# The first feed-forward product of layer 2 in seven block products instead of eight

## The chip, the cores and the metric

The kernel runs on one core of a Trainium2 chip. A core has a matrix engine (TensorE, PE in the profile), a vector engine (VectorE, DVE), a scalar engine (ScalarE, ACT), a general engine (GpSimd, POOL) and a queue that issues transfers (SyncE, SP). The metric is the device time of one execution in microseconds (us), lower is better. Each time is a median over several executions.

## The reference

One inference step of a trunk with two layers, over 512 sample tokens and 128 prompt tokens of width 1024. Each layer has a mixer (layer 1: gated DeltaNet and Hyena, layer 2: two kinds of attention) and then a gated feed-forward part, which is what the change touches in layer 2:

```python
D_MODEL, D_FF = 1024, 2816

def conv_ffn(h, w_up, conv_w, conv_b, w_down):
    a, b = jnp.split(h @ w_up, 2, axis=-1)
    a = dwconv(a, conv_w, conv_b)            # three taps along the tokens
    return (jax.nn.silu(a) * b) @ w_down

        h = rmsnorm(x, p['norm_ffn'][i]) * (1.0 + sc2) + sh2
        x = x + g2 * conv_ffn(h, p['ffn_w_up'][i], ...)
    y = rmsnorm(x, p['final_norm'])
```

"The first feed-forward product" is `h @ w_up`: 640 tokens by 1024 features, times 1024 by 5632 weights. All inputs are float32.

## The kernel before

Everything is feature-major: features on the 128 partitions, tokens along the free axis, in 642 columns (512 sample tokens, two zero columns, 128 prompt tokens). The tokens are worked in two halves, of 384 and 258 columns (`HALVES`; `CHALVES` has 384 and 260, with the neighbours that a three-tap convolution needs). 1024 features are eight tiles of 128, called d or k.

Float32 products are made of three float32r products: an operand is split into a high part (ScalarE casts it, L295) and a low part (VectorE subtracts, L296), and `mm3` (L301 to L303) adds high x high, high x low and low x high. So a weight block of 1024 x 128 (a "w", 512 KB, loaded by SP into one of three buffers named `wr`) costs one cast and one subtraction, and its product with a half of the tokens costs 8 x 3 = 24 matmuls. There is room for four split weights, two pools of two.

`ffn` (L469 to L505) goes over 22 tiles of 128 columns of D_FF, in three groups of 8, 7 and 7 (`FGROUPS`). In each tile (I call it a unit) it makes the a part and the b part of `h @ w_up` (96 matmuls: for a and for b, for either half, 24), convolves a on ScalarE (L512) and VectorE (L518), applies SiLU on ScalarE (L490), multiplies by b on VectorE (L492), and splits the result into `g` (cast on ScalarE L494, subtraction on GpSimd L495). After a group, `project_out` (L434 to L464) adds the group's part of the second product to the residual stream x.

The input of `ffn` comes from the `project_out` before it, that of the mixer. Its last four feature tiles are done for the first half of the tokens and then for the second. While the second is being multiplied, the first half's norm is computed (`norm_stats` L363, `norm_mod` L390 to L403: L394 normalises on VectorE, L400 scales on ScalarE, L402 and L403 split into `h3h` and `h3l`, the low parts on VectorE and GpSimd by turns). The second half's norm follows. `ffn` covers it: it begins with the first half's products of two units (`firsts`, L476), 96 matmuls of 384 columns, and only then needs the second half.

The code is recorded by a framework that assigns each tile its buffer, orders the instructions of each engine once, when the program is built, and adds the semaphores. On the chip ScalarE, VectorE and GpSimd each work through a fixed list in order, and so do TensorE's products. A product group accumulates in one of the eight banks of PSUM (three named "mm", one "s", four "d").

## Time and profile before

| | |
|---|---|
| median of 3 runs | 1935.4 us (1934.53 to 1935.5) |
| the profiled execution, span | 1938.0 us |
| of it: TensorE busy | 1856.1 us |
| VectorE busy | 1168.4 us |
| ScalarE busy | 705.3 us |
| GpSimd busy | 390.2 us |
| first matmul of layer 2's `ffn` | at 1449.54 us |

The profile is of one execution. Its span is 2.6 us above the median of the three timed runs. No time outside the span is listed. A row of a timeline has the start, the duration, the engine, the source line, and what it writes and reads; x2 means that two instructions stand in one row. A row of the groups by line ends with the busy time, the mean duration of one in ns, and the idle time of the engine before them with what ended it. Matmuls overlap in the pipeline, so the step from one to the next is read from their starts, not from their durations.

### The profile page before, as it was taken

How to read it: one execution, taken by the hardware profiler on the slowest of the kernel's cores; microseconds unless marked ns; L12 is line 12 of the kernel's file. 1: busy time of each engine (PE TensorE's matmuls, PEld its weight loads, DVE VectorE, ACT ScalarE, POOL GpSimd, SP SyncE). 2: the span in 40 equal slices, each digit the busy share in tenths (PEclk: the TensorE clock that was granted, in tenths of full speed). 3: DMA queues.
4: the chain of work that ended last, by engine and by line, in shares of the span. 5: the costliest groups of instructions: out<-in, count | busy, mean ns of one | idle time of the engine just before them, and what ended most of it. 6: DMA issues, size and time to landing. Idle time of an engine off the chain costs nothing. (4 is left out here: it accounts for less than half of the span.)

```text
span 1938.0 us, 31344 instructions
## 1 busy us (share of the span) xinstructions
PE 1856.1 (96%) x12512; PEld 1735.8 (90%) x12512; DVE 1168.4 (60%) x2416; ACT 705.3 (36%) x1304; POOL 390.2 (20%) x403
## 2 busy tenths in 40 slices
PE   5899999999888999999999999999999999999998
PEld 1578999998667999999999998978799999999997
DVE  5755666667887669757677648655655433333334
ACT  3555443343222263312312224544435322322332
POOL 2323332324554011101100104310002100110111
PEclk9899999999989999999999999999999999999999
DMA  8321112116552435434344223201212222222221
GB/s 288 126 101 66 44 57 78 56 63 209 167 165 91 142 134 192 135 128 142 119 153 131 70 89 108 82 25 47 88 55 87 68 75 77 74 69 77 74 67 55
DMA packets 66188, 197.48 MB, mean 102 GB/s; under 512 B 6872, under 2 KB 18520, under 8 KB 65914
## 3 DMA queue, kind: packets, MB, share of 16 engines
q1 hardware_dynamic: 52000, 176.71, 28.0%
q10 hardware_dynamic: 14042, 18.76, 2.8%
q8 instruction: 99, 1.62, 0.3%
q14 instruction: 47, 0.39, 0.1%
HBM read 178.91 MB, written 16.54 MB: 101 GB/s over the span
## 5 line engine op out<-in xcount | busy, mean ns | idle before, releaser
L295 ACT CAST wwh<-wr 128x1024 fp32r<-128x1024 f32 (+1 forms) x180 | 185.3, 1029 | 455.2 <-PE mm L302 444.5
L296 DVE TENSOR_TENSOR wwl<-wr,wwh 128x1024 fp32r<-128x1024 f32 (+1 forms) x180 | 221.8, 1232 | 106.8 <-ACT wwh L295 106.7
L302 PE MATMUL mm<-h1l,wwh 128*128 128x384 f32 (+2 forms) x704 | 219.7, 312 | 0.9 <-DVE h1l L403 0.9
L302 PE MATMUL mm<-h3l,wwh 128*128 128x384 f32 (+2 forms) x704 | 219.1, 311 | 0.9 <-DVE h3l L403 0.9
L303 PE MATMUL mm<-h1h,wwl 128*128 128x384 f32 (+2 forms) x704 | 219.5, 312 | 0.0
L301 PE MATMUL mm<-h1h,wwh 128*128 128x384 f32 (+2 forms) x704 | 219.0, 312 | 0.0
L303 PE MATMUL mm<-h3h,wwl 128*128 128x384 f32 (+2 forms) x704 | 218.9, 311 | 0.0
L301 PE MATMUL mm<-h3h,wwh 128*128 128x384 f32 (+2 forms) x704 | 218.3, 311 | 0.0
L518 DVE SCALAR_TENSOR_TENSOR cv<-mm,par,cv 128x259 f32<-128x259 f32 (+3 forms) x272 | 148.6, 548 | 112.9 <-ACT cv L512 110.2
L419 DVE SCALAR_TENSOR_TENSOR x<-mm,mod,x 128x128 f32<-128x128 f32 (+1 forms) x192 | 78.5, 436 | 180.8 <-PE mm L303 180.7
L247 DVE SCALAR_TENSOR_TENSOR mjunk<-mraw,crow 128x512 f32<-128x512 f32 x192 | 150.0, 793 | 2.7 <-ACT crow L235 1.5
L301 PE MATMUL mm<-h0h,wwh 128*128 128x384 f32 (+2 forms) x448 | 148.8, 332 | 0.5 <-DVE d L642 0.2
L302 PE MATMUL mm<-h0l,wwh 128*128 128x384 f32 (+2 forms) x448 | 140.8, 314 | 0.0
L303 PE MATMUL mm<-h0h,wwl 128*128 128x384 f32 (+2 forms) x448 | 139.7, 312 | 0.0
L302 PEld LDWEIGHTS mm<-h1l,wwh 128*128 128x128 f32 x704 | 133.6, 190 | 1.8 <-DVE h1l L403 1.6
L302 PEld LDWEIGHTS mm<-h3l,wwh 128*128 128x128 f32 x704 | 133.1, 189 | 1.8 <-DVE h3l L403 1.6
L303 PEld LDWEIGHTS mm<-h1h,wwl 128*128 128x128 f32 x704 | 133.4, 189 | 0.0
L301 PEld LDWEIGHTS mm<-h1h,wwh 128*128 128x128 f32 x704 | 133.0, 189 | 0.2 <-ACT h1h L402 0.2
L301 PEld LDWEIGHTS mm<-h3h,wwh 128*128 128x128 f32 x704 | 132.8, 189 | 0.2 <-ACT h3h L402 0.2
L303 PEld LDWEIGHTS mm<-h3h,wwl 128*128 128x128 f32 x704 | 132.8, 189 | 0.0
L512 ACT ACTIVATE cv<-mm,par 128x383 f32<-128x383 f32 (+1 forms) x136 | 73.8, 542 | 149.5 <-PE mm L303 144.0
L492 DVE TENSOR_TENSOR fs<-mm,fs 128x384 f32<-128x384 f32 x88 | 42.8, 490 | 98.6 <-PE mm L303 97.6
(462 smaller groups left out, 4657.9 us busy)
## 6 DMA issues: line engine op xcount, KB each, us to landing
wr<-in_w_up SPq DMA_DIRECT2D x88, 512.0 KB, 3.3
wr<-in_w_mod SPq DMA_DIRECT2D x48, 512.0 KB, 4.8
mraw<-in_w_modT SPq DMA_DIRECT2D x48, 512.0 KB, 3.8
wr<-in_w_in SPq DMA_DIRECT2D x28, 512.0 KB, 3.3
wr<-in_w_dn SPq DMA_DIRECT2D x32, 448.0 KB, 3.3
wr<-in_w_out SPq DMA_DIRECT2D x16, 512.0 KB, 3.3
wr<-in_w_dn SPq DMA_DIRECT2D x16, 512.0 KB, 3.6
wr<-in_od_w_in SPq DMA_DIRECT2D x16, 512.0 KB, 3.9
```

What stands on the lines that cost most here:

```text
L247: nc.vector.scalar_tensor_tensor(out=junk, in0=raw[:, c], scalar=1.0, in1=rows[m][:, c], op0=ALU.mult, op1=ALU.mult, accum_out=part[:, d, ...
L295: nc.scalar.copy(hi[:, :K], src)
L296: nc.vector.tensor_tensor(out=lo[:, :K], in0=src, in1=hi[:, :K].bitcast(F32), op=ALU.subtract)
L301: nc.tensor.matmul(ps, l[0](k), r[0](k), start=start, stop=False)
L302: nc.tensor.matmul(ps, l[0](k), r[1](k), start=False, stop=False)
L303: nc.tensor.matmul(ps, l[1](k), r[0](k), start=False, stop=stop)
L419: nc.vector.scalar_tensor_tensor(out=xt[:, a:b], in0=ps[:, a - c0 : b - c0], scalar=mcol(layer, ch, d, m), in1=xt[:, a:b], op0=ALU.mult, o ...
L492: nc.vector.tensor_tensor(out=s[:, a:b], in0=ps[:, : b - a], in1=s[:, a:b], op=ALU.mult)
L512: nc.scalar.activation(t[:, o0:o1], p[:, o0 - a : o1 - a], AF.Identity, scale=w[1], bias=0.0 if bias is None else bias)
L518: nc.vector.scalar_tensor_tensor(out=t[:, c0:c1], in0=p[:, c0 + s_ - a : c1 + s_ - a], scalar=w[i], in1=t[:, c0:c1], op0=ALU.mult, op1=ALU ...
```

## The change

In layer 2 alone, `h` (tokens by features) is taken as 2 x 2 blocks: 320 columns of tokens (0 to 319, or 320 to 511 and the prompt) by four feature tiles. The weights of a unit are 2 x 2 blocks as well: the upper and lower 512 rows of the a part (w11, w21) and of the b part (w12, w22). In place of the eight block products, seven are made, of sums and differences of blocks on either side. Each block product is 4 x 3 = 12 matmuls of 320 columns, so a unit has 84 matmuls.

- `norm_blocks` replaces `norm_mod` here: it normalises as before, scales into four raw blocks (a11, a12, a21, a22), splits a11 and a12 with the first half, and with the second half forms s1 to s4 in four VectorE operations for each k, and splits s1 to s4 and a22. A product of a11 or a12 needs the first half alone. All others need the second.
- `block_weights` splits seven 512 x 128 operands of a unit, and makes four sums of weight blocks on VectorE. Two operands share the room of one split weight, so eight fit.
- `up_unit` makes the seven products in the order a11, a12, s2, s1, s3, s4, a22, in three banks: X takes a11, s2, s3 and a22, one added to the other; V takes s1 and s4; Y takes a12. Between two products into one bank ScalarE copies the running sum out (`keep`: q1, u2, q5, u3). VectorE (two) and GpSimd (two) add the copies up into `ar` and `br`.
- `give` does what followed in `ffn`: the convolution now reads `ar` from SBUF and is three instructions of 641 or 642 columns, in place of six on the halves.
- `ffn_blocks` loops over the units; it begins with a11 and a12 of the first two units.
- `ys` (the output's tiles) are allocated later, tile by tile. `mm3` has a flag that changes no instruction. A scratch size of the build is set to 1024. Comments are dropped, which moves lines: `mm3` is L304 to L306 after the change.

```diff
+SPARTS = (((0, 320, 0),), ((320, 512, 0), (PO, NT, 192)))
+ST = 320
...
+        def split(self, n, k, src, eng=None):
+            if n not in self.hi:
+                self.hi[n], self.lo[n] = (slot(n + t_, (P, 4, ST), F32R) for t_ in "hl")
+            h_ = self.hi[n][:, k, :]
+            nc.scalar.copy(h_, src)
+            (eng or nc.vector).tensor_tensor(out=self.lo[n][:, k, :], in0=src, in1=h_.bitcast(F32), op=ALU.subtract)
...
+    def norm_blocks(x, rb, layer, w, B, hf):
...
+            nc.vector.tensor_tensor(out=t[:, c0:c1], in0=x[d // 2][:, d % 2, c0:c1], in1=rb[:, c0:c1], op=ALU.mult)
...
+                        nc.scalar.activation(
+                            to[:, o + a_ - a : o + b_ - a], t[:, a_:b_], AF.Identity,
+                            scale=scl[:, layer, w, d, m : m + 1], bias=mcol(layer, 0 if w == 0 else 3, d, m),
+                        )
+        if hf == 0:
+            for d in range(KD):
+                norm(d)
+                n = ("a11", "a12")[d // 4]
+                B.split(n, d % 4, B.raw(n, d % 4), nc.vector if d % 2 == 0 else nc.gpsimd)
+            return
+        for k in range(4):
+            norm(k)
+            norm(k + 4)
+            a11, a12, a21, a22 = (B.raw(n, k) for n in ("a11", "a12", "a21", "a22"))
+            s1 = tmp.tile([P, NT], F32, tag="fs", name=nm("s1"))[:, :ST]
+            nc.vector.tensor_tensor(out=s1, in0=a22, in1=a21, op=ALU.subtract)
+            nc.vector.tensor_tensor(out=a11, in0=a11, in1=a21, op=ALU.subtract)
+            nc.vector.scalar_tensor_tensor(out=a21, in0=a11, scalar=-1.0, in1=a22, op0=ALU.mult, op1=ALU.subtract)
+            nc.vector.scalar_tensor_tensor(out=a12, in0=a21, scalar=-1.0, in1=a12, op0=ALU.mult, op1=ALU.subtract)
+            for n, src in (("s2", a21), ("s1", s1), ("s3", a11), ("s4", a12), ("a22", a22)):
+                B.split(n, k, src)
...
+    def split_op(src):
+        hi, lo = op_room()
+        nc.scalar.copy(hi, src)
+        nc.vector.tensor_tensor(out=lo, in0=src, in1=hi.bitcast(F32), op=ALU.subtract)
...
+    def block_weights(a, b, pool):
+        TT = nc.vector.tensor_tensor
+        w11, w21, w12, w22 = a[:, :4], a[:, 4:], b[:, :4], b[:, 4:]
+        yield split_op(w11)
+        yield split_op(w21)
+        TT(out=w11, in0=w11, in1=w12, op=ALU.add)
+        t2 = pool.tile([P, 4, 128], F32, tag="t2", name=nm("t2"), bufs=1)
+        TT(out=t2, in0=w11, in1=w22, op=ALU.add)
+        yield split_op(t2)
+        yield split_op(w11)
+        TT(out=w12, in0=w12, in1=w22, op=ALU.add)
+        yield split_op(w12)
+        yield split_op(w22)
+        TT(out=w21, in0=w21, in1=t2, op=ALU.add)
+        yield split_op(w21)
...
+        def product(ps, n, st):
+            w = next(ws)
+            for k in range(4):
+                mm3(ps[:, :ST], w, B.of(n), k, st and k == 0, k == 3, not st)
...
+        X, Y = bank("d", "bx"), bank("mm", "by")
+        product(X, "a11", True)
+        q1 = keep("q1", X)
+        product(Y, "a12", True)
+        yield
+        nc.vector.tensor_tensor(out=ar[:, :ST], in0=Y[:, :ST], in1=q1, op=ALU.add)
+        product(X, "s2", False)
+        u2 = keep("u2", X)
+        V = bank("d", "bv")
+        product(V, "s1", True)
+        q5 = keep("q5", V)
+        product(X, "s3", False)
+        u3 = keep("u3", X)
+        for a, b, o in SPARTS[1]:
+            nc.gpsimd.tensor_tensor(out=br[:, a:b], in0=u3[:, o : o + b - a], in1=q5[:, o : o + b - a], op=ALU.add)
+        product(V, "s4", False)
+        nc.vector.tensor_tensor(out=br[:, :ST], in0=V[:, :ST], in1=u2, op=ALU.add)
+        product(X, "a22", False)
+        for a, b, o in SPARTS[1]:
+            nc.scalar.copy(ar[:, a:b], X[:, o : o + b - a])
+        give(f, ar, br)
...
+            def give(f, ar, br):
...
+                nc.scalar.activation(t, ar, AF.Copy, scale=w[1])
+                for c0, c1, s_, i in ((1, NT, -1, 0), (0, NT - 1, 1, 2)):
+                    nc.vector.scalar_tensor_tensor(
+                        out=t[:, c0:c1], in0=ar[:, c0 + s_ : c1 + s_], scalar=w[i], in1=t[:, c0:c1], op0=ALU.mult, op1=ALU.add
+                    )
...
+                nc.scalar.activation(s, t, AF.Silu, bias=pc("ffn_conv_b", layer * NF + f))
+                nc.vector.scalar_tensor_tensor(out=s, in0=s, scalar=-1.0, in1=br, op0=ALU.mult, op1=ALU.mult)
+                k = f - f0
+                nc.scalar.copy(g.h(k, 0, NT), s)
+                nc.gpsimd.tensor_tensor(out=g.l(k, 0, NT), in0=s, in1=g.h(k, 0, NT).bitcast(F32), op=ALU.subtract)
...
-    h = Act("h3", gap=False)
-    take, pre = into(x, 1, 1, h)
-    project_out(x, mix, 1, 2, wout(1), KD, take)
-    ys = [slot("y") for _ in range(4)]
...
+    project_out(x, mix, 1, 2, wout(1), KD, lambda hf, rb: norm_blocks(x, rb, 1, 1, hb, hf))
+    ys = []
...
-    ffn(x, h, 1, final, pre, post=scaled)
+    ffn_blocks(x, hb, 1, final, scaled, gstack)
```

Up to the norm of layer 2's feed-forward part, the lists of all engines are the same instructions in the same order as before. Two places differ in a way that the prediction uses.

The first is VectorE's list at the second half's norm. Before, it reads (nt is the normalised tile, x the residual stream, rb the reciprocals, h3l the low parts of the input):

```order
L394 TENSOR_TENSOR nt_14628<-x_14016,rb_14033 128x258
L394 TENSOR_TENSOR nt_14634<-x_14016,rb_14033 128x258
L394 TENSOR_TENSOR nt_14640<-x_14017,rb_14033 128x258
L394 TENSOR_TENSOR nt_14646<-x_14017,rb_14033 128x258
L403 TENSOR_TENSOR h3l_14025<-nt_14628,h3h_14024 128x258
```

After, it reads (cwl is a weight operand's low part, a11r to a22r the raw blocks, s_2445 the tile of s1):

```order
L509 TENSOR_TENSOR nt_14664<-x_14018,rb_14028 128x258
L551 TENSOR_TENSOR cwl_14861<-wr_14746,cwh_14860 128x512
L533 TENSOR_TENSOR a11r_14500<-a11r_14500,a21r_14502 128x320
L532 TENSOR_TENSOR s_2445_14635<-a22r_14530,a21r_14502 128x320
L551 TENSOR_TENSOR cwl_14897<-wr_14744,cwh_14896 128x512
L534 SCALAR_TENSOR_TENSOR a21r_14502<-a11r_14500,a22r_14530 128x320
L533 TENSOR_TENSOR a11r_14500<-a11r_14500,a21r_14502 128x320
L535 SCALAR_TENSOR_TENSOR a12r_14528<-a21r_14502,a12r_14528 128x320
L497 TENSOR_TENSOR s2l_14641<-a21r_14502,s2h_14640 128x320
L532 TENSOR_TENSOR s_2458_14668<-a22r_14530,a21r_14502 128x320
L497 TENSOR_TENSOR s1l_14645<-s_2445_14635,s1h_14644 128x320
```

Twelve operations of VectorE (eight L394, four L403) have become 44 on the second half (eight L509, four each of L532 to L535, twenty L497), with three low parts of weights among them.

The second is in the middle of a group, on ScalarE. Before, a unit's list is six rows (cv and fs are the convolution and SiLU, mm is PSUM, wwh a weight's high part, g10h the high part of the unit's result):

```order
L512 ACTIVATE cv_15170<-mm_15064,par 128x383
L295 CAST wwh_15310<-wr_15308 128x1024
L512 ACTIVATE cv_15170<-mm_15089,par 128x259
L490 ACTIVATE fs_15177<-cv_15170,par 128x642
L295 CAST wwh_15366<-wr_15364 128x1024
L494 CAST g10h_14701<-fs_15177 128x642
```

After, it is sixteen; these are twelve of them in a row (q, u are the copies of `keep`, bx and bv the banks X and V, t_2596 the sum t2):

```order
L584 COPY q_2575_15465<-bx_15449 128x320
L550 CAST cwh_15590<-wr_15584 128x512
L629 ACTIVATE fs_15440<-cv_15436,par 128x642
L632 CAST g10h_14740<-fs_15440 128x642
L584 COPY u_2579_15501<-bx_15449 128x320
L550 CAST cwh_15626<-wr_15584 128x512
L550 CAST cwh_15626<-t_2596_15624 128x512
L584 COPY q_2583_15520<-bv_15503 128x320
L550 CAST cwh_15662<-wr_15586 128x512
L584 COPY u_2584_15537<-bx_15449 128x320
L550 CAST cwh_15662<-wr_15586 128x512
L550 CAST cwh_15698<-wr_15584 128x512
```

The SiLU (L629) and the cast (L632) in it belong to the unit before, and they wait for VectorE; the copies (L584) that TensorE needs stand behind them, and one of them (q_2583) behind the cast of t2.

More of the change, by code (lines that the diff above doesn't have):

```diff
@@ new lines, in norm_blocks, with norm @@
+    def norm_blocks(x, rb, layer, w, B, hf):
+        c0, c1 = HALVES[hf]
+        def norm(d):
+            k, f = d % 4, d // 4
+            t = tmp.tile([P, NT], F32, tag="ft" if d % 2 else "fs", name=nm("nt"))
+            nc.vector.tensor_tensor(out=t[:, c0:c1], in0=x[d // 2][:, d % 2, c0:c1], in1=rb[:, c0:c1], op=ALU.mult)
+            for i, parts in enumerate(SPARTS):
+                to = B.raw((("a11", "a12"), ("a21", "a22"))[i][f], k)
+                for a, b, o in parts:
+                    a_, b_ = max(a, c0), min(b, c1)
+                    if a_ < b_:
+                        m = 0 if a < PO else 1
+                        nc.scalar.activation(
[19 more added lines that the diff above has]
+                B.split(n, k, src)
@@ new lines, in up_unit, with keep @@
+    def up_unit(layer, f, B, pool, outs, give):
+        def product(ps, n, st):
+            w = next(ws)
+            for k in range(4):
+                mm3(ps[:, :ST], w, B.of(n), k, st and k == 0, k == 3, not st)
+        def keep(s_, ps):
+            q = pool.tile([P, ST], F32, tag=s_, name=nm(s_), bufs=2)
+            nc.scalar.copy(q, ps[:, :ST])
+            return q
+        ws = block_weights(load_raw(A["w_up"][layer, f], KD), load_raw(A["w_up"][layer, NF + f], KD), pool)
+        ar, br = (outs[f % 2][:, i, :] for i in range(2))
+        X, Y = bank("d", "bx"), bank("mm", "by")
[19 more added lines that the diff above has]
+        give(f, ar, br)
@@ new lines, in ffn_blocks @@
+    def ffn_blocks(x, B, layer, then, post, gstack):
+        gpool = B.pool
+        pool = gstack.enter_context(tc.tile_pool(name=f"b{layer}", bufs=2))
+        outs = [slot("ab") for _ in range(2)]
+        for t_ in outs:
+            nc.gpsimd.memset(t_[:, :, 512:514], 0.0)
+        for gi, (f0, n) in enumerate(FGROUPS):
+            g = Act(f"g{layer}{gi}", 4, gpool, gap=False)
+            def give(f, ar, br):
+                t = tmp.tile([P, NT], F32, tag="ft", name=nm("cv"))
+                w = [pc("ffn_conv_w", layer * 3 * NF + f + i * NF) for i in range(3)]
+                nc.scalar.activation(t, ar, AF.Copy, scale=w[1])
[3 more added lines that the diff above has]
+                    )
+                s = tmp.tile([P, NT], F32, tag="fs", name=nm("fs"))
+                nc.scalar.activation(s, t, AF.Silu, bias=pc("ffn_conv_b", layer * NF + f))
[3 more added lines that the diff above has]
+                nc.gpsimd.tensor_tensor(out=g.l(k, 0, NT), in0=s, in1=g.h(k, 0, NT).bitcast(F32), op=ALU.subtract)
+                step()
+            us = [up_unit(layer, f, B, pool, outs, give) for f in range(f0, f0 + n)]
+            for u in us[:2] if f0 == 0 else ():
+                next(u)
+            for u in us:
+                for _ in u:
+                    pass
+            project_out(
+                x, g, layer, 5,
+                lambda d, f0=f0, n=n: A["w_dn"][layer, d][:, 128 * f0 : 128 * (f0 + n)],
+                n, *((then, post) if gi == len(FGROUPS) - 1 else (None, None)),
+            )
+        gstack.close()
@@ L1968, in build @@
     import concourse.bacc as bacc
-    nc = bacc.Bacc("TRN2", target_bir_lowering=False, num_devices=1)
+    nc = bacc.Bacc("TRN2", target_bir_lowering=False, num_devices=1, dynamic_dma_scratch_size=1024)
     A = {
```

31 lines of the change are left out of this document (25 added, 6 removed).

## The prediction

> **What bounds the kernel now.** I read the page's busy times first, then the waits of TensorE from the mixer's last product to the end, and then one unit of `ffn` as a window, from the same point of one unit to that of the next.
>
> ```profile
> span 1938.0 us, 31344 instructions
> PE 1856.1 (96%) x12512; PEld 1735.8 (90%) x12512; DVE 1168.4 (60%) x2416; ACT 705.3 (36%) x1304; POOL 390.2 (20%) x403
> ```
>
> ```profile
> PE rb L379 <- POOL nr L184: 2.4, 2, 1.3
> PE ss L372 <- ACT sq L410: 1.1, 1, 1.1
> PE mm L302 <- DVE h3l L403: 0.9, 2, 0.6
> ```
>
> ```profile
> 1511.03:1525.29 14.26, 14.26 (x98) 14.26 (x97) 5.56 (x8) 4.52 (x7) 1.74 (x1) 1.00 0.23 74
> ```
>
> Over 558 us the longest waits of TensorE are 4.4 us together. A unit takes 14.26 us, all of it TensorE; VectorE works 5.56 us of it and ScalarE 4.52. So fewer columns through TensorE shorten the unit, for as long as the other engines keep up. What one matmul costs is read from starts:
>
> ```profile
> 1600.54 0.28 PE L301 MATMUL mm<-g10h,wwh 128*128 128x258 f32 x1
> ...
> 1603.42 0.34 PE L301 MATMUL mm<-g10h,wwh 128*128 128x384 f32 x1
> ...
> 1605.88 0.34 PE L303 MATMUL mm<-g10h,wwl 128*128 128x384 f32 x1
> ```
>
> 24 matmuls of 258 columns start within 2.88 us, 0.120 us each; then 14 of 384 within 2.46 us, 0.176 us each. That is 0.442 ns a column and 6 ns beside it, so 320 columns take 0.147 us. No floor shows down to 258 columns, hence none is to be feared at 320.
>
> **The units on TensorE.** 84 matmuls x 0.1474 = 12.38 us in place of 14.26. For 22 units this saves 41.4 us if nothing else is late: the bound on the good side.
>
> **The units on the other engines.** The prices:
>
> ```profile
> 1442.69 1.03 DVE L394 TENSOR_TENSOR nt<-x,rb 128x384 f32<-128x384 f32 x2 [0.67 <-ACT rb L383]
> 1526.27 1.23 DVE L296 TENSOR_TENSOR wwl<-wr,wwh 128x1024 fp32r<-128x1024 f32 x1 [0.53 <-ACT wwh L295]
> L492 DVE TENSOR_TENSOR fs<-mm,fs 128x384 f32<-128x384 f32 x22 | 12.3, 557 | 25.4 <-PE mm L303 24.5 <-ACT fs L490 0.9
> L247 DVE SCALAR_TENSOR_TENSOR mjunk<-mraw,crow x192: 673/682/2096, 717.9 to 1091.0; 128x512 f32<-128x512 f32 x192
> ```
>
> VectorE: two of 384, of 0.56 us each, stand in 1.03, so one begins 0.47 after the other and they overlap by 0.09; one of 1024 is 1.23, so 1.14 to the next; between them 1.05 ns a column. 512 columns are then 0.60 us. The product-and-add of 512 is 0.68, so 0.82 for 641. A unit has seven low parts and four sums (11 x 0.60 = 6.6), three product-and-adds (2.5) and two sums out of PSUM of 320 columns (0.45 each, from the 557 ns for 384): 10.0 us in place of 5.56.
>
> ```profile
> 1460.98 1.27 ACT L400 ACTIVATE nt<-nt,mod,scl 128x128 f32<-128x128 f32 x3 [0.50 <-DVE nt L394]
> 1448.88 0.93 ACT L402 CAST h3h<-nt 128x384 fp32r<-128x384 f32 x2
> L295 ACT CAST wwh<-wr 128x1024 fp32r<-128x1024 f32 x52 | 54.5, 1048 | 157.4 <-PE mm L302 157.4
> L512 ACT ACTIVATE cv<-mm,par 128x383 f32<-128x383 f32 x22 | 12.8, 581 | 53.1 <-PE mm L303 52.3 <-POOL h3l L403 0.8
> L490 ACT ACTIVATE fs<-cv,par 128x642 f32<-128x642 f32 x22 | 18.3, 833 | 37.5 <-DVE cv L518 37.5
> ```
>
> ScalarE: seven casts of 512 (0.55 each, between the 384 and the 1024), four copies of 320 out of PSUM (0.5), two short ones (0.35) and three of 642 (0.8): 9.0 us. Both fit into 12.38 us by their sums. But GpSimd and VectorE do not work side by side freely:
>
> ```profile
> 1463.70 0.64 POOL L403 TENSOR_TENSOR h3l<-nt,h3h 128x258 fp32r<-128x258 f32 x1 [4.46 <-ACT h3h L402]
> 1452.18 1.23 POOL L403 TENSOR_TENSOR h3l<-nt,h3h 128x384 fp32r<-128x384 f32 x1 [1.11 <-ACT h3h L402]
> ...
> 1454.21 1.01 POOL L403 TENSOR_TENSOR h3l<-nt,h3h 128x384 fp32r<-128x384 f32 x1 [0.66 <-ACT h3h L402]
> 1526.94 1.98 POOL L495 TENSOR_TENSOR g10l<-fs,g10h 128x642 fp32r<-128x642 f32 x1 [12.52 <-ACT g10h L494]
> ```
>
> ```profile
> 1452.61 1.89 DVE L296 TENSOR_TENSOR wwl<-wr,wwh 128x1024 fp32r<-128x1024 f32 x1
> 1454.42 1.22 DVE L403 TENSOR_TENSOR h3l<-nt,h3h 128x384 fp32r<-128x384 f32 x1
> ```
>
> The low part at 1452.61, begun while GpSimd was at work, took 1.89 us, not 1.23; the next, begun 0.21 us into GpSimd's, 1.22, not 0.56. GpSimd's at 1526.94 took 1.98 us, but VectorE's of 1526.27 ended at 1527.50, 1.42 before its end. So the later one waits for the earlier. The Trainium skill states this (page SBUF — State Buffer, section Who interferes with whom): an instruction of VectorE with two SBUF inputs and one of GpSimd that reads SBUF exclude each other, and "the other **fully blocks**"; the trace agrees (1.89 against 1.23 us). By that rule the sum is the one below, without it that of the first rival. GpSimd has 1.42 us for `g`, and 0.5 and 0.4 for its two parts of `br` (from the 0.64): 2.3 us a unit that VectorE cannot use. 10.0 + 2.3 = 12.3 us, as much as TensorE needs.
>
> Both lists are worked in order, so I walked them through two units with these durations, each instruction beginning when the one ahead of it and its inputs are done. In the first unit all copies of `keep` are out just before TensorE writes the bank again, the copies q5 and u2 with nothing to spare. In the second, GpSimd's `g` comes between two sums of VectorE, t2 is done 1.3 us later, ScalarE's cast of t2 waits for it, and q5 behind that cast is ready 0.9 us after TensorE wanted the bank V for s4. The pair takes 25.7 us: 12.9 us a unit. Bounds: 12.4 (GpSimd takes its turn where VectorE waits anyway), and 14.0 if every wait at the head of VectorE's list adds up (below). I take 12.9, the walk's. Gain: 22 x (14.26 - 12.9) = 29.9 us.
>
> Transfers stay 1 MB a unit on SP, in the same order; a weight buffer is now kept until its last sum, but in the walk it is free about 4 us before its successor is read, and a load lands in 3.3 us:
>
> ```profile
> wr<-in_w_up SPq DMA_DIRECT2D x88, 512.0 KB, 3.3
> ```
>
> **The start.** Before:
>
> ```profile
> 1449.54 0.34 PE L301 MATMUL mm<-h3h,wwh 128*128 128x384 f32 x1
> ...
> 1470.77 0.28 PE L301 MATMUL mm<-h3h,wwh 128*128 128x260 f32 x1
> ```
>
> ```profile
> 1460.51 1.44 DVE L394 TENSOR_TENSOR nt<-x,rb 128x258 f32<-128x258 f32 x4 [1.82 <-ACT rb L387]
> ...
> 1469.06 0.43 DVE L403 TENSOR_TENSOR h3l<-nt,h3h 128x258 fp32r<-128x258 f32 x1 [1.73 <-ACT h3h L402]
> ```
>
> From 1449.54 to 1470.77 TensorE has 96 matmuls of the first half, 16.9 us of work in 21.2, so 4.3 us are lost. Under this cover the second half's norm runs from 1460.51 to 1469.5. After the change the cover is 48 matmuls of 320, 7.1 us, while the norm grows: eight normalisations (0.36 each), sixteen sums (0.42), twenty low parts (0.42), three weight parts (0.60) and a sum out of PSUM make 20.3 us of VectorE. ScalarE has 16 scalings of 128 (0.42) and 20 casts of 320 (0.38), 14 us beside it. The norm starts no sooner than 1460.5, since x and its reciprocals come as before; s2 and s1 are whole at about 1480. By then TensorE has had 72 matmuls, 10.6 us of 30.7: 20.1 us lost, 15.8 more than before. A bound below is 12 (VectorE in 16 us, the rest of s2 and s1 sooner), above 25 (each low part also waits for its cast).
>
> TensorE's clock after such a hole:
>
> ```profile
> 511.44 1.09 PE L801 MATMUL tr<-ident,dx 128*128 128x128 f32 x4 [4.14 <-DVE dx L939]
> ```
>
> ```profile
> 508.00:510.00 2.00, 0.00 (x0) 0.00 (x0) 2.00 (x3) 0.00 (x0) 2.00 (x3) 0.98 0.90 277
> 510.00:512.00 2.00, 0.56 (x3) 0.59 (x4) 2.00 (x3) 0.00 (x0) 2.00 (x2) 0.50 0.00 0
> ...
> 514.00:516.00 2.00, 2.00 (x6) 1.58 (x5) 0.84 (x3) 0.00 (x0) 0.00 (x0) 0.50 0.65 147
> 516.00:518.00 2.00, 2.00 (x15) 1.82 (x14) 0.00 (x0) 0.60 (x2) 0.00 (x0) 0.82 0.63 246
> ```
>
> After a gap of 4.1 us the granted clock (third figure from the end) is 0.50 until about 516.7, 5 us into the work that follows. The hole at the start is longer, so about 2.5 us of TensorE go there. The Trainium skill (page TensorE: Matmul & The Clock Gate, section What's actually happening) gives half rate until a window of 3.4 us has been busy; by that alone I estimate 1.7 to 3.4 us, which would move the sum by under 1 us. The trace agrees with the half rate.
>
> **The ends of the three groups.**
>
> ```profile
> L302 PEld LDWEIGHTS mm<-g11l,wwh 128*128 128x128 f32 x112 | 21.1, 189 | 0.4 <-POOL g11l L495 0.4
> ```
>
> In the second group the next product waits 0.4 us for the last unit's low part. After the change the last product (a22) is copied, convolved whole, and split only then: 0.7 + 0.8 + 2 x 0.85 + 0.85 + 0.85 + 0.75 + 1.45 + 0.7 between engines = 7.8 us. The products that do not need it cover 44 matmuls (6.6 us) in the first group, 38 (5.7 us) in the others. I take 0.8 us more each, 2.5 together.
>
> **Sum.** -29.9 + 15.8 + 2.5 + 2.5 = -9.1 us: 1938.0 becomes 1928.9, and from the median 1935.4 it is 1926.3.
>
> **Rivals.**
>
> *TensorE stays the bound of every unit.* GpSimd's work falls where VectorE waits anyway. For it: in the walk VectorE still has about 1.6 us without work in a unit, ahead of the convolution. Against it: 12.3 us of 12.4 leave no room for order. 12.4 us a unit: -40.9 + 20.8 = -20.1, 1915.3.
>
> *VectorE's list sets the unit, and the change is slower.* Place: VectorE, between the sum of s4 and the convolution, where it waits about 1.7 us for the product a22, its copies and the scaled copy. If the operands' room is already used up and nothing later in the list can pass, a unit is 10.0 + 2.3 + 1.7 = 14.0 us. The gain is 5.7, the price 20.8: +15.1, 1950.5. It decides from 13.3 us a unit on (14.26 - 20.8/22). For it: the list is fixed and the sums are tight. Against it: eight operands of room let VectorE work six products ahead.
>
> *The start eats the gain.* If every low part waits for its cast, 20 x 0.45 = 9 us come on top of the start: -0.1, 1935.3.
>
> **How the numbers follow.** My forecast 0.44, TensorE as the bound 0.23, VectorE as the bound 0.20, the start 0.13. About 0.2% (3.9 us) can be told from no change. Faster: nine tenths of the first, the second, and a little of the last: 0.65. Slower: the third and some of the last: 0.23. Same: 0.12. The range reaches below the first rival by the start's lower bound of 12 (1912) and takes in half of the slower case (1945); the forecast alone would be 1919 to 1934.
>
> **What would show it.** Right: a unit's window of 12.7 to 13.2 us, TensorE waiting in every second one for the copy q5 out of V and not for weights; VectorE over 80% busy in it; TensorE nearly without work from about 1457 to 1466, sparse to 1480, and then some us at a clock of 0.50. Wrong: units of 12.4, units above 13.3, or a start whose hole is not near 20 us.

## The result and the profile after

The changed kernel takes 1924.8 us in the median of four runs (1924.36 to 1925.47), the kernel before 1935.3 (1934.53 to 1935.5): a ratio of 0.9945, with an interval of 0.9931 to 0.9959. It is faster by 0.55%, which is clear of the interval, and the forecast was 1926.3. The page of the profile after begins so:

```profile
span 1922.7 us, 31316 instructions
PE 1821.7 (95%) x12248; PEld 1694.0 (88%) x12248; DVE 1311.0 (68%) x2624; ACT 791.1 (41%) x1544; POOL 424.0 (22%) x445
```

TensorE has 34 us less to do, VectorE 143 us more. Where the time went is read from windows that begin with the first matmul of each stage. The rows are, in turn: the units of the first group, the output product of that group, the same two for the second group and for the third. The first figure behind the stretch is its length; the one behind POOL's is the granted clock.

```profile
1443.42:1570.69 127.27, 111.89 (x683) 105.39 (x681) 112.10 (x180) 84.76 (x178) 29.48 (x28) 0.91 0.23 76
1570.69:1628.84 58.15, 57.48 (x387) 56.84 (x385) 24.01 (x40) 11.46 (x16) 1.32 (x1) 1.00 0.19 63
1628.84:1717.99 89.15, 87.43 (x591) 86.31 (x590) 76.03 (x104) 53.75 (x104) 20.47 (x20) 1.00 0.26 86
1717.99:1769.38 51.39, 50.41 (x339) 49.77 (x338) 23.01 (x40) 10.49 (x15) 1.56 (x1) 1.00 0.19 58
1769.38:1858.72 89.34, 87.33 (x591) 86.28 (x589) 76.54 (x105) 53.70 (x105) 22.49 (x24) 1.00 0.28 92
1858.72:1922.70 63.98, 54.18 (x362) 52.87 (x360) 28.13 (x55) 23.97 (x51) 10.12 (x7) 0.93 0.18 62
```

The same six stages of the kernel before:

```profile
1449.54:1567.89 118.35, 116.09 (x778) 114.65 (x777) 55.54 (x87) 50.80 (x85) 20.47 (x19) 1.00 0.25 80
1567.89:1624.78 56.89, 56.89 (x386) 56.89 (x385) 19.46 (x31) 9.03 (x9) 1.74 (x1) 1.00 0.23 75
1624.78:1724.62 99.84, 99.84 (x675) 99.84 (x674) 38.68 (x57) 30.69 (x41) 10.84 (x6) 1.00 0.23 71
1724.62:1774.85 50.23, 50.11 (x339) 49.79 (x337) 18.78 (x31) 8.49 (x9) 1.78 (x1) 1.00 0.26 82
1774.85:1874.68 99.83, 99.83 (x675) 99.83 (x674) 38.69 (x57) 30.69 (x41) 10.86 (x6) 1.00 0.23 70
1874.68:1938.00 63.32, 53.88 (x362) 52.88 (x360) 26.33 (x53) 21.83 (x47) 10.35 (x7) 0.94 0.17 57
```

| stage of layer 2's feed-forward | before | after | difference |
|---|---|---|---|
| units of the first group (8) | 118.35 | 127.27 | +8.92 |
| its output product | 56.89 | 58.15 | +1.26 |
| units of the second group (7) | 99.84 | 89.15 | -10.69 |
| its output product | 50.23 | 51.39 | +1.16 |
| units of the third group (7) | 99.83 | 89.34 | -10.49 |
| its output product and the end | 63.32 | 63.98 | +0.66 |
| together | 488.46 | 479.28 | -9.18 |

The stage is 9.2 us shorter: 21 us are won in the units of two groups, 9 are lost in those of the first, and 3 in the output products. The spans of the two profiles differ by 15.3 us, but 6.1 of that lie ahead of the change, where the two kernels have the same instructions: the first product begins at 1449.54 in one and at 1443.42 in the other. In the profiles of the experiments below it begins anywhere from 1441.9 to 1451.8. So I compare the kernels below by this stage as well as by their times. Two profiles of one and the same kernel, in which VectorE makes all low parts, gave 463.83 and 463.74 us for it. Where GpSimd makes a part of a12, the stage is less steady, by up to 1.6 us; the reason is under "The start".

**The units.** Two units next to each other, each from its first product (a11) to that of the next:

```profile
1506.86:1520.26 13.40, 12.58 (x86) 12.32 (x85) 12.92 (x18) 8.07 (x16) 3.79 (x4) 1.00 0.22 78
1520.26:1532.75 12.49, 12.49 (x87) 12.30 (x86) 10.93 (x16) 8.53 (x17) 3.21 (x3) 1.00 0.26 85
```

In the first two groups units of 12.3 to 12.5 and 13.1 to 13.4 us take turns, once the start is over; in the third they are 12.3 to 13.1 us without such an order, and one is 13.8. In the longer ones of the first two TensorE waits for the copy q out of the bank V, ahead of the product s4, as the walk had it:

```profile
1516.64 0.41 PE L304 MATMUL bv<-s4h,cwh 128*128 128x320 f32 x1 [0.82 <-ACT q L584]
```

GpSimd's row and VectorE's rows just before show why:

```profile
1513.26 1.80 POOL L633 TENSOR_TENSOR g10l<-fs,g10h 128x642 fp32r<-128x642 f32 x1 [6.17 <-ACT g10h L632]
```

```profile
1512.93 0.68 DVE L560 TENSOR_TENSOR wr<-wr,wr 128x512 f32<-128x512 f32 x1
1513.65 1.95 DVE L562 TENSOR_TENSOR t<-wr,wr 128x512 f32<-128x512 f32 x1
```

The sum t has 512 columns like the one ahead of it, and takes 1.95 us in place of 0.68: GpSimd had begun the gate's low part 0.39 us earlier and was done at 1515.06. ScalarE's cast of t, and behind it the copy q, come late by the same 1.3 us.

**The start.** TensorE's rows from a low part of a12 to the second half's first operands, VectorE's row at the second half's sums of squares (ss), and then the windows of that place:

```profile
1449.68 0.57 PE L305 MATMUL by<-a12l,cwh 128*128 128x320 f32 x1 [1.78 <-POOL a12l L497]
...
1457.31 0.31 PE L306 MATMUL by<-a12h,cwl 128*128 128x320 f32 x1
1462.49 0.64 PE L304 MATMUL bx<-s2h,cwh 128*128 128x320 f32 x1 [4.88 <-ACT s2h L496]
```

```profile
1455.24 0.16 DVE L377 TENSOR_SCALAR nv<-ss 128x2 f32<-128x2 f32 x1 [3.97 <-PE ss L373]
```

```profile
1447.00:1451.00 4.00, 2.22 (x11) 1.96 (x11) 3.21 (x6) 3.17 (x9) 3.46 (x2) 0.85 0.00 0
1451.00:1455.00 4.00, 4.00 (x24) 4.00 (x22) 0.27 (x1) 1.57 (x4) 0.00 (x0) 0.73 0.00 0
1455.00:1459.00 4.00, 1.75 (x11) 1.23 (x11) 3.14 (x8) 2.06 (x6) 1.16 (x3) 1.00 0.00 0
1459.00:1463.00 4.00, 0.51 (x2) 0.43 (x2) 3.87 (x9) 3.92 (x11) 0.00 (x0) 0.63 0.47 145
1463.00:1467.00 4.00, 3.79 (x11) 2.43 (x11) 4.00 (x11) 2.78 (x8) 0.00 (x0) 0.50 0.31 117
1467.00:1471.00 4.00, 0.68 (x2) 0.28 (x2) 4.00 (x12) 2.70 (x8) 0.00 (x0) 0.50 0.00 0
1471.00:1475.00 4.00, 3.04 (x7) 1.84 (x7) 4.00 (x11) 3.59 (x11) 0.00 (x0) 0.50 0.00 0
1475.00:1479.00 4.00, 3.92 (x13) 3.20 (x13) 4.00 (x9) 2.76 (x6) 0.00 (x0) 0.50 0.01 2
```

The 48 products of the first half are done at 1457.6, the 24 of s2 and s1 at 1477.1. VectorE begins the second half's norm at 1457.82 and is busy from there on, 4.00 us of 4.00 in each of the last four rows; TensorE waits, or works at a granted clock of 0.50. From 1443.42 to 1477.07 it had 72 x 0.147 = 10.6 us of work: 23.1 us lost.

The norm itself begins late, 14.4 us after the first product. The sums of squares that it needs stand behind products of a12 in TensorE's list. TensorE waited 1.78 us there for GpSimd's low part of a12, the 13 matmuls from 1449.68 to 1453.23 started 0.27 us apart in place of 0.147, and VectorE waited 3.97 us for the sums. The wait comes in each profile in which GpSimd makes this part, the half clock behind it does not: here and in two of the experiments below (the one with the fill, and the two passes with the gate on VectorE) the norm begins 14.4 us after the first product, in three others (the gate on VectorE, the gate made twice, the two passes alone) 12.8 to 12.9, with full clock. So in such profiles 1.6 us of the stage can be the run's and not the kernel's.

What TensorE waits for from the mixer's last products to the end, the longest waits first (in all, times, longest):

```profile
PE bx L304 <- ACT s2h L496: 4.9, 1, 4.9
PE bv L304 <- ACT s1h L496: 4.2, 2, 3.4
PE bv L304 <- ACT q L584: 3.8, 7, 0.8
PE bx L304 <- ACT u L584: 2.6, 2, 1.4
PE by L305 <- POOL a12l L497: 1.8, 1, 1.8
...
PE mm L305 <- POOL g11l L633: 0.7, 1, 0.7
...
```

### The profile page after: what moved, and what is told of

Its sections match the earlier page's. It is cut to its first block, busy times and chain, and to the rows that moved or that the text cites. A ratio compares the mean times of both kernels' runs of the same rounds, so it can differ in the third digit from the quotient of the medians.

```text
span 1922.7 us, 31316 instructions
## 1 busy us (share of the span) xinstructions
PE 1821.7 (95%) x12248; PEld 1694.0 (88%) x12248; DVE 1311.0 (68%) x2624; ACT 791.1 (41%) x1544; POOL 424.0 (22%) x445
## 5 line engine op out<-in xcount | busy, mean ns | idle before, releaser
L306 PE MATMUL mm<-h1h,wwl 128*128 128x384 f32 (+2 forms) x704 | 218.9, 311 | 0.0
L304 PE MATMUL mm<-h1h,wwh 128*128 128x384 f32 (+2 forms) x704 | 218.5, 311 | 0.0
L299 DVE TENSOR_TENSOR wwl<-wr,wwh 128x1024 fp32r<-128x1024 f32 (+1 forms) x136 | 167.6, 1233 | 60.3 <-ACT wwh L298 60.1
L304 PE MATMUL mm<-h0h,wwh 128*128 128x384 f32 (+2 forms) x448 | 148.9, 332 | 0.5 <-DVE d L823 0.2
L306 PE MATMUL mm<-h0h,wwl 128*128 128x384 f32 (+2 forms) x448 | 139.4, 311 | 0.0
L699 DVE SCALAR_TENSOR_TENSOR cv<-mm,par,cv 128x382 f32<-128x382 f32 (+3 forms) x184 | 100.2, 546 | 57.2 <-ACT cv L693 56.1
L306 PEld LDWEIGHTS mm<-h1h,wwl 128*128 128x128 f32 x704 | 132.9, 189 | 0.0
L304 PEld LDWEIGHTS mm<-h1h,wwh 128*128 128x128 f32 x704 | 132.6, 188 | 0.2 <-ACT h1h L405 0.2
L550 ACT CAST cwh<-wr 128x512 fp32r<-128x512 f32 x132 | 79.5, 622 | 79.8 <-PE mm L305 23.2
L551 DVE TENSOR_TENSOR cwl<-wr,cwh 128x512 fp32r<-128x512 f32 x132 | 99.4, 772 | 12.5 <-ACT cwh L550 12.4
L304 PE MATMUL od<-owh,h2h 128*128 128x256 f32 x320 | 98.4, 308 | 0.4 <-ACT h2h L405 0.4
L1112 POOL TENSOR_TENSOR am<-a,msk 128x512 fp32r<-128x512 f32 x60 | 73.0, 1225 | 91.9 <-PE Q L1141 81.3
L306 PE MATMUL od<-owh,h2l 128*128 128x256 f32 x320 | 90.5, 286 | 1.9 <-DVE h2l L406 1.1
L305 PE MATMUL od<-owl,h2h 128*128 128x256 f32 x320 | 90.7, 284 | 0.0
L693 ACT ACTIVATE cv<-mm,par 128x383 f32<-128x383 f32 x92 | 50.6, 550 | 94.5 <-PE mm L306 89.7
L304 PEld LDWEIGHTS mm<-h0h,wwh 128*128 128x128 f32 x448 | 85.4, 191 | 3.1 <-issue 1.8
```

Of the source, the lines that this page charges most:

```text
L299: nc.vector.tensor_tensor(out=lo[:, :K], in0=src, in1=hi[:, :K].bitcast(F32), op=ALU.subtract)
L304: nc.tensor.matmul(ps, l[0](k), r[0](k), start=start, stop=False, skip_group_check=more)
L305: nc.tensor.matmul(ps, l[0](k), r[1](k), start=False, stop=False, skip_group_check=more)
L306: nc.tensor.matmul(ps, l[1](k), r[0](k), start=False, stop=stop, skip_group_check=more)
L550: nc.scalar.copy(hi, src)
L551: nc.vector.tensor_tensor(out=lo, in0=src, in1=hi.bitcast(F32), op=ALU.subtract)
```

## The experiments

My theory: a unit's length is set by VectorE and by the GpSimd instructions that read SBUF, which exclude VectorE's two-input instructions while they run; the start is lost to VectorE's norm, for which the new order leaves too little cover. The rivals: TensorE or the order of VectorE's list sets the units and GpSimd is beside the point; and the start is lost to something else that would stay without the norm. The times of the kernel before in the three groups of runs were 1938.19, 1937.86 and 1937.31 us, so results stand as ratios to it; the changed kernel is 0.9945. The expectations of the first four were written in the times of the first runs (changed kernel 1924.8).

**The gate's low part on VectorE.** In place of GpSimd, VectorE makes the low part of the gate and the two sums for the second half of br.

```
-            nc.gpsimd.tensor_tensor(out=br[:, a:b], in0=u3[...], in1=q5[...], op=ALU.add)
+            nc.vector.tensor_tensor(out=br[:, a:b], in0=u3[...], in1=q5[...], op=ALU.add)
...
-                nc.gpsimd.tensor_tensor(out=g.l(k, 0, NT), in0=s, ...)
+                nc.vector.tensor_tensor(out=g.l(k, 0, NT), in0=s, ...)
```

> The kernel after, with the low part of g and the two parts of br made on VectorE in place of GpSimd. VectorE gets 1.3 us more work in each unit. Theory (exclusion): VectorE has 11.3 us with nothing to exclude it, against 12.3 now; units fall from 12.8 to 12.4 or 12.5, the ends of the groups lose 0.6 us each: 1924.8 becomes 1915 (1912 to 1918). Rival (VectorE's own list, or ScalarE's order, sets the unit): more work on VectorE makes the unit longer by up to 1.3 us, or leaves it: 1925 to 1953.

Measured: 1915.07 us, 0.9882 (0.9865 to 0.9898), and 466.65 us of feed-forward, 12.6 less than the changed kernel. A unit:

```profile
1519.00:1531.32 12.32, 12.32 (x87) 12.32 (x85) 12.00 (x21) 7.69 (x16) 0.00 (x0) 1.00 0.25 86
```

Behind the start all units but one in the last group are now 12.3 us, TensorE without a gap; the one is 13.4 us, with a wait of VectorE for a load of weights of 1.56 us in it. Of the 12.6 us, 4.8 lie in the units of the second and third group, 5.2 in those of the first and 2.6 behind the groups. Up to 1.6 of the first group's can be the half clock behind a12's wait, which the changed kernel's profile has and this one's has not; the times, 12.2 us apart by ratios, don't rest on these two profiles. VectorE got more to do and was yet sooner done. The sums t by themselves, of the changed kernel and of this one (1500 to 1560):

```profile
L562 DVE TENSOR_TENSOR t<-wr,wr 128x512 f32<-128x512 f32 x5 | 7.0, 1397 | 0.1
```

```profile
L562 DVE TENSOR_TENSOR t<-wr,wr 128x512 f32<-128x512 f32 x5 | 3.4, 687 | 0.1
L633 DVE TENSOR_TENSOR g10l<-fs,g10h 128x642 fp32r<-128x642 f32 x5 | 4.1, 819 | 0.0
```

VectorE makes the gate's low part in 0.82 us; GpSimd needed 1.6 to 1.8, and VectorE's instruction beside it took up to 1.3 us longer. The theory holds.

**The gate's low part made twice by GpSimd.**

```
                 nc.gpsimd.tensor_tensor(out=g.l(k, 0, NT), in0=s, ...)
+                nc.gpsimd.tensor_tensor(out=g.l(k, 0, NT), in0=s, ...)
```

> The kernel after, with GpSimd's subtraction for the low part of g made twice in each unit (the same result). GpSimd is busy for about 3.5 us of a 12.8 us unit and nothing waits for its result but the end of a group. Theory (GpSimd and VectorE exclude each other): VectorE loses 1.4 us more in each unit, 10.0 + 3.7 = 13.7 us of it no longer fit, units go from 12.8 to 13.4 to 14.2, and the time from 1924.8 to about 1942 (1938 to 1955). Rival (the units' excess over 12.4 comes from ScalarE's order alone): units stay at 12.8; only the ends of the three groups get 1.4 us longer, 1929.

Measured: 1948.21 us, 1.0055 (1.0039 to 1.0071), 499.16 us of feed-forward, 19.9 more (though without the half clock behind a12's wait). GpSimd was busy 3.2 to 3.8 us of a unit's 12.5 to 13.4, so it had time for a second one. VectorE had not:

```profile
1518.82 1.95 DVE L562 TENSOR_TENSOR t<-wr,wr 128x512 f32<-128x512 f32 x1
1520.70 2.05 DVE L565 TENSOR_TENSOR wr<-wr 128x512 f32<-128x512 f32 x1
```

Two instructions are held up in place of one, and most units are 13.3 to 15.0 us long. With one GpSimd instruction more the change would have been slower than the kernel before: the rival on the other side lay that near.

**The same move in the kernel before.** As a control, the eight-product kernel with the gate's low part of this layer on VectorE.

```
-                nc.gpsimd.tensor_tensor(out=g.l(k, 0, NT), ...)
+                (nc.vector if layer else nc.gpsimd).tensor_tensor(out=g.l(k, 0, NT), ...)
```

> The kernel before (eight products) with the low part of the gate in the second layer made by VectorE in place of GpSimd. The theory, that the place of this subtraction matters only where VectorE's list is full: no change, 0.999 to 1.001, since VectorE works 5.6 of 14.26 us of a unit there. The rival: GpSimd's slow subtraction costs each kernel the same 12 us, and the gain of the version on VectorE has nothing to do with the seven products: 0.993 to 0.995.

Measured: 1935.88 us, 0.9991 (0.998 to 1.0001), 489.29 us of feed-forward against 488.46. No change can be told. Who makes this subtraction matters only since seven products filled VectorE's list.

**A GpSimd instruction that only writes.**

```
+                nc.gpsimd.memset(junk, 0.0)
                 nc.gpsimd.tensor_tensor(out=g.l(k, 0, NT), in0=s, ...)
```

> The changed kernel with one more GpSimd instruction in each unit, which only writes: a fill of 642 columns with zeros into a buffer that nobody reads, ahead of the low part of the gate. The theory, that an instruction of GpSimd that reads SBUF and one of VectorE with two inputs exclude each other, expects no cost for one that reads nothing: within 0.2% of the changed kernel (ratio 0.993 to 0.996 to the kernel before). The rival: any work of GpSimd holds VectorE up, for as long as it lasts: about 1 us a unit, 20 us in all or half of the second subtraction's 21, a ratio of 0.999 to 1.005.

Measured: 1927.7 us, 0.994 (0.9928 to 0.9952), 479.53 us of feed-forward. That number tells less than it seems: the fills wait for nothing, and all 22 were placed far ahead of the units, at 1389 us. But there they stood beside VectorE, and its rows with two SBUF inputs answer the question by themselves, though for two forms only, and not in the units.

```profile
1389.36 15.19 POOL L634 MEMSET junk<- 128x642 f32 x22 [36.18 <-PE o L1902]
```

```profile
1397.16 1.23 DVE L299 TENSOR_TENSOR wwl<-wr,wwh 128x1024 fp32r<-128x1024 f32 x1 [0.35 <-ACT wwh L298]
...
1400.40 0.56 DVE L416 TENSOR_TENSOR acc<-acc,sq 128x384 f32<-128x384 f32 x1 [0.59 <-ACT sq L413]
```

GpSimd fills without a break for 15 us, and VectorE's subtraction of 1024 columns keeps its 1.23 us, its sum of 384 its 0.56. So it is not any work of GpSimd that holds VectorE up. The Trainium skill (page SBUF — State Buffer, section Who interferes with whom) says that a VectorE instruction with two SBUF inputs contends with a GpSimd instruction that reads SBUF, "not with one that only writes it"; these rows agree.

**The second half's norm in two passes.** s2 and s1 of all four k first, then the sum for s4 and the parts of s3, s4 and a22.

```
...
             nc.vector.scalar_tensor_tensor(out=a21, in0=a11, scalar=-1.0, in1=a22, ...)
+            for n, src in (("s2", a21), ("s1", s1)):
+                B.split(n, k, src)
+        for k in range(4):
+            a11, a12, a21, a22 = (B.raw(n, k) for n in ("a11", "a12", "a21", "a22"))
             nc.vector.scalar_tensor_tensor(out=a12, in0=a21, scalar=-1.0, in1=a12, ...)
-            for n, src in (("s2", a21), ("s1", s1), ("s3", a11), ("s4", a12), ("a22", a22)):
+            for n, src in (("s3", a11), ("s4", a12), ("a22", a22)):
                 B.split(n, k, src)
```

> The kernel after, with the second half's norm in two passes: first s2 and s1 for all four k, then s3, s4 and a22. The same operations, in another order. Theory (the hole at the start is TensorE waiting for VectorE's s2 and s1, which are whole only at the end of 20 us of VectorE): s2 and s1 are whole after 13 us, TensorE does 24 matmuls beside the rest, the hole shrinks by 4 to 8 us: about 1919 (1916 to 1921). Rival (the hole is as long as VectorE's work, in any order, or is the clock's): 1924 to 1926.

Measured: 1927.84 us, 0.9948 (0.9934 to 0.9963), 477.92 us of feed-forward against 479.28. My expectation fell. The products of s2 and s1 are through 6.4 us sooner after the first product (1.6 of that because this profile has no half clock behind a12's wait), but the time is waited elsewhere; the waits of the first group:

```profile
PE bx L304 <- ACT s2h L496: 4.9, 1, 4.9
PE bx L304 <- ACT u L588: 2.1, 3, 1.2
...
PE bx L304 <- ACT q L588: 1.4, 1, 1.4
PE bv L304 <- ACT s1h L496: 1.0, 1, 1.0
...
PE bx L304 <- ACT cwh L554: 0.7, 1, 0.7
```

The wait for s1 fell from 4.2 to 1.0 us; in its place TensorE waits for the copies u and q of the first units and for the weights of the second (cwh), which stand behind the norm in the lists of ScalarE and VectorE. The units behind the first two become 13.1 to 14.6 us long, against 12.5 to 14.1. The 1.4 us by which the stage is shorter are no more than the half clock that this profile lacks.

**Without the norm of the second half.** This kernel leaves out the second half's normalisation and the sums and parts of s1 to s4 and a22, whose products read a11 and a12 in their place.

```
-        for k in range(4):
+        for k in range(0):
...
+            n = {"s2": "a11", "s1": "a12", "s3": "a11", "s4": "a12", "a22": "a11"}.get(n, n)
```

> The kernel after without the second half's norm and without the sums of blocks (left out: s1 to s4 and a22 are never formed; their products read a11 and a12 in their place), so that all 22 units can begin on the first half's norm. Theory: the hole at the start goes. From the first product to the start of the third unit it takes 49.4 us now, and 2 x 12.4 + 5 = 30 then: 1924.8 becomes about 1905 (1902 to 1908), and the units after it stay at 12.8. Rival (the start is bound by the splitting of the first units' weights, or by the clock): less than half of that, 1915 or above.

Measured: 1911.14 us (1903.97 to 1915.29), 0.986 (0.9835 to 0.9884); by ratios 16.4 us less than the changed kernel. The theory had 20, which its interval still takes in (0.9835 is 21.3 us less). The units of the first group:

```profile
1451.79:1560.99 109.20, 102.78 (x683) 99.78 (x681) 95.34 (x136) 70.85 (x142) 30.72 (x26) 1.00 0.27 88
```

109.20 us against 127.27, at a clock of 1.00 against 0.91: 18.1 us of the start's loss go with the norm and its sums, and with the clock; up to 1.6 of them are the half clock behind a12's wait. The other 6.7 over eight units of 12.81 us stay: among them 1.8 us for a12's low part and 3.3 for the copies u and q.

**Both at once, and the rest of GpSimd's part.** Two kernels on top of the one with the gate on VectorE: one with the two passes, one in which VectorE makes all low parts of a11 and a12 too.

```
-                B.split(n, d % 4, B.raw(n, d % 4), nc.vector if d % 2 == 0 else nc.gpsimd)
+                B.split(n, d % 4, B.raw(n, d % 4), nc.vector)
```

> The kernel in which VectorE makes the low parts of the gate and the GpSimd sums, and in which the second half's norm makes the operands s2 and s1 of all four k first, in a pass of their own. The theory: with GpSimd left in, the earlier s2 and s1 brought nothing because VectorE was behind its work for the first units anyway; without GpSimd's share VectorE has about 2 us to spare in each unit, TensorE sets the units, and a hole shorter by 6 us comes through: 0.9882 of the kernel before less 4 to 6 us, 0.985 to 0.986, the first group about 118 us from its first product to the first product of its output in place of 122.0. The rival: the backlog after the hole belongs to the order of VectorE's list (the first unit's weight parts behind the norm) and not to GpSimd: 0.988 to 0.989, the first group 121 to 123 us.

> The kernel in which VectorE makes the low parts of the gate and the GpSimd sums, and now also the low parts of a12 of the first half, which GpSimd made. TensorE waited 1.79 us for one of them, and the sums of squares of the second half (product with ones) stand behind these products in TensorE's list although their input was ready 1.9 us before. The theory: the wait goes, the second half's reciprocal comes earlier by it, and the whole norm with it: less 1.0 to 1.9 us, a ratio of 0.9872 to 0.9877. The rival: a wait ahead of a longer wait costs nothing, the hole just begins earlier: 0.988 to 0.989.

Measured, two passes: 1911.66 us, 0.9867 (0.9854 to 0.9881), between the two expectations; but 466.53 us of feed-forward, where one pass had 466.65. The theory's 4 to 6 us don't come, with GpSimd gone either. How much does come this pair can't say: the profile with two passes has the half clock behind a12's wait and that with one has not, so up to 1.6 us may be hidden. Measured, all low parts on VectorE: 1910.34 us, 0.9855 (0.9842 to 0.9868), 463.83 us of feed-forward, 2.8 less than the 466.65 (neither profile has the half clock there). That is more than the 1.0 to 1.9 expected: the first product of s2 begins 14.7 us after the first product of all, against 17.5. The wait of 1.8 us had stood ahead of the sums of squares in TensorE's list, and with it the start of the norm: 10.0 us after the first product, against 12.8.

**The clock kept up, and the two passes once more.** 96 (80 beside the two passes) more matmuls of a11 by itself, into a bank that nobody reads, in the hole.

```
...
+        def warm(m):
+            for _ in range(m):
+                h = B.of("a11")[0](0)
+                nc.tensor.matmul(J[:, :ST], h[:, :128], h, start=True, stop=True)
...
```

> The kernel with every low part of the feed-forward on VectorE (the gate's, the sums br, and those of a12), and 96 more matmuls of TensorE in the hole at the start of the first group: 32 ahead of the first unit's product of s2, and 8 behind each of the eight steps of s2 and s1, which multiply a11 by itself into a bank that nobody reads. In all 14.1 us of work at full clock, in the 15.6 us that TensorE waits or works at half clock there. The theory, that the half clock after the hole costs what the prediction put down for it: the granted clock stays above 0.9 from the hole on, and s3, s4 and what follows run at full speed at once, 2.0 to 2.8 us less than without the extra matmuls: ratio 0.984 to 0.9845, the feed-forward 461.0 to 461.9 us in its profile in place of 463.8. The rival: VectorE's backlog sets the pace after the hole, so a faster TensorE only waits: 0.985 to 0.987, 463 to 464 us.

> The kernel with every low part of the feed-forward on VectorE, and the second half's norm in two passes, s2 and s1 of all four k first. With the low parts of a12 on GpSimd the two passes gave nothing in the profile (466.5 us of feed-forward against 466.7), though TensorE waited 3 us less for the operands: 1.5 us of that went to a half clock after the 1.8 us wait for GpSimd's a12, and 1.1 us to the first unit's weights, which were split late. The theory, that part of the loss was the clock's: without that wait 1 to 3 us less than the kernel in one pass, 461 to 463 us of feed-forward, ratio 0.984 to 0.985. The rival, that VectorE's total work up to the third unit sets the pace whatever comes first in it: 463 to 465 us, 0.985 to 0.987.

> Both together: every low part of the feed-forward on VectorE, the second half's norm in two passes, and 80 extra matmuls in the hole (32 ahead of s2, 6 behind each of the eight steps). If the clock's loss and the order's loss are separate, both gains come: 459 to 461 us of feed-forward, ratio 0.983 to 0.984. The rival, that VectorE's backlog is behind both: 463 to 464 us, 0.985 to 0.987.

> The kernel with every low part of the feed-forward on VectorE once more, as the level for the runs beside it on the same chip: 0.9842 to 0.9868 as in its first run, 463.8 us of feed-forward (463.3 to 464.8). No theory expects anything else.

| kernel, all low parts on VectorE | us | ratio, interval | feed-forward |
|---|---|---|---|
| as it is, again | 1913.59 | 0.9879, 0.986 to 0.9898 | 463.74 |
| with more matmuls | 1909.84 | 0.9854, 0.9833 to 0.9875 | 460.45 |
| in two passes | 1912.35 | 0.9867, 0.9849 to 0.9884 | 463.08 |
| both | 1911.04 | 0.9856, 0.9835 to 0.9877 | 462.30 |

The times don't tell these four apart, since their intervals overlap; the profiles tell a little more. The units of the first group with more matmuls, and without them:

```profile
1445.15:1562.46 117.31, 115.36 (x779) 113.69 (x777) 109.36 (x204) 84.51 (x176) 1.17 (x3) 1.00 0.26 82
```

```profile
1444.17:1563.16 118.99, 108.15 (x682) 103.75 (x681) 109.42 (x204) 84.55 (x176) 1.16 (x3) 0.91 0.25 81
```

The clock is 1.00 all the way, and the stage 1.7 us shorter, somewhat under the 2.0 to 2.8 expected. Another 1.3 us of the 3.3 lie in the third group, where one unit of 13.6 us is 12.32 here. In that unit VectorE waits 1.80 us for a load of weights in one profile without the extra matmuls and 1.78 in the other, and here not at all; that the extra matmuls have a part in it I can't show. The two passes give 0.7 us (463.08 against 463.74), in the one pair whose profiles both have no wait for GpSimd's a12. Both together give less than the matmuls alone: TensorE then waits 1.4 us for the cast of the next units' weights and 0.9 for their low part. Whether the extra matmuls shorten the kernel stays open at the size of these intervals.

## Why the prediction was right, and where its terms were off

The sum was -9.1 us and the stage gave -9.18; the median fell by 10.5. The direction and the places of the gain and of the losses came out, but for a late norm and a late load (below). That the total fits to 0.1 us is more than the terms deserve, since two of them erred against each other:

| term | predicted | measured | how it is read |
|---|---|---|---|
| 22 units | -29.9 | -31.9 | mean of 12.81 us where units follow each other, against 14.26 |
| start and clock | +18.3 | +20.5 | first group: 127.27 less 8 x 12.81, against 118.35 less 8 x 14.26; 18.8 of it the longer hole, 1.6 the clock behind it |
| ends of the groups | +2.5 | +3.1 | output products: +1.26, +1.16, +0.66 |
| not in the sum | 0 | -0.9 | second and third group: together shorter by 0.9 than 14 x 12.81 would make them |

**The units.** The walk with GpSimd's exclusion was right in size (a pair of 25.6 us against 25.7) and in place (every second unit of the first two groups, the copy q out of V, ahead of s4; the third group has no such order). It put 2.3 us a unit down to GpSimd's share; by the mean times of VectorE's rows between 1500 and 1560 us, against those of the kernel with the gate on VectorE, it is 1.8: in five units 5 x 0.71 for t, 5 x 0.54 for the last sum (L568), and 29 x 0.09 for the low parts of the weights. The bound below, 12.4 us, is what the units take with GpSimd out of the way, 12.33.

**The start.** The hole was put at 20.1 us and was 23.1. VectorE's part was sized well: from 1457.82 to 1477.25 it worked 19.4 us with hardly a gap, where the sum had 20.3. What is over lies ahead of the norm. The prediction let it begin 11.0 us after the first product (1460.5 less 1449.54), "since x and its reciprocals come as before"; it began 14.4 us after it. The reciprocals don't come as before: their sums of squares stand behind a12's products, and these waited 1.8 us for GpSimd and then ran at half clock for 3.5 us, neither of which the prediction priced. The half clock there, 1.6 us, was this run's (see "The start" above): without it the stage would, by my estimate, have been up to 1.6 us shorter than the sum said. The 2.5 us for the clock after the hole were too many by 0.9: the twelve matmuls from 1477.07 to 1480.43 lost 1.6 us, and 1.7 come back where the clock is kept up.

**Transfers** were taken at nothing, since a buffer was free 4 us before its successor is read in the walk. In one unit that cost time. VectorE waits nine times for a load of weights, 6.5 us in all, and behind the longest wait the SiLU and the copy u come late too, so TensorE waits:

```profile
1836.81 0.69 DVE L560 TENSOR_TENSOR wr<-wr,wr 128x512 f32<-128x512 f32 x1 [1.94 <-DMA wr<-in_w_up]
1841.01 0.41 PE L304 MATMUL bx<-s3h,cwh 128*128 128x320 f32 x1 [1.25 <-ACT u L584]
```

This is the unit of 13.8 us in the third group; the load for it was issued at 1832.2 and landed more than 4 us later. Behind the other eight loads no such wait of TensorE is shown.

**The rivals.** That TensorE bounds every unit is what GpSimd prevented (12.33 us without it, but for the one unit with the load). That VectorE's list makes the change slower needed 13.3 us a unit: with a second GpSimd subtraction the units take 13.8 in the mean and the kernel is slower than before. Both were real, and the prediction stood between them because GpSimd's share was near that of the walk (1.8 us against 2.3). That the low parts at the start each wait for their cast is not seen: VectorE is busy 4.00 us of 4.00 there.

**What I got wrong behind it** was the belief that the hole could be made cheaper by order. The norm and the first units' weights are one list of VectorE's, and bringing s2 and s1 forward sends the weights back by as much. Three pairs of profiles show 1.4, 0.1 and 0.7 us for it, where 4 to 8, 4 to 6 and 1 to 3 were hoped for. In the first two pairs one profile of the two has the half clock behind a12's wait, so each is uncertain by 1.6 us; the third has no such difference.

A version that beats both kernels comes out of this: the change with every low part of the feed-forward on VectorE, 0.9855 (0.9842 to 0.9868) of the kernel before in one group of runs and 0.9879 (0.986 to 0.9898) in another, against 0.9945 for the change as it was made. From the kernel with only the gate and the sums on VectorE (0.9882, 0.9865 to 0.9898) the times don't tell it apart; the stage does, by 2.8 us.

## What to carry to other kernels

When work moves off the engine that bounds a kernel onto one that has room, add to that engine's sum what its neighbour takes from it, not only its own instructions: GpSimd's subtraction (1.8 us) cost nothing that could be told with VectorE 40% busy, but GpSimd's part of the units cost 11 to 12.6 us with VectorE 85 to 88% busy in their stages, and giving that part to the full engine itself was the cheaper choice. Walk the lists through two units, not one, and look at the stage where the work starts apart from the stage where it repeats. A wait at the start that is made of one engine's total work yielded 0.7 us to reordering here; what brought it forward was taking away a wait that stood ahead of it (2.8 us).
